# First products of gate and up: sums on VectorE, twelve early chunks, a late state update, and projection weights kept in DRAM as split pairs

## The chip, the cores and the metric

The kernel runs on one core of one Trainium2 chip. The metric is the device time of one execution in microseconds (us). Before the change it is 1289.85 us, the median of three runs (1289.18 to 1289.87).

## The reference, cut to what matters

One layer of a decoder is computed for 1024 new tokens of one sequence and for 8 running sequences of 4 tokens each, 1056 tokens in all, in float32:

```
proj = einsum('bld,dp->blp', h, w_in)                    # 1024 -> 2824 columns
o_a, S_new = gated_delta_rule(q, k, v, g, beta, S0)      # 4 heads, recurrent state S
o_b, k_new, v_new = swa_sinks(...)                       # sliding window, 8 query heads
m = concat[rmsnorm_gated(o_a, z), o_b] @ w_out
x = layernorm(ALPHA * x + m)                             # "LN1"
gate, up = split(x @ w_ffn_in)                           # 2 x 2816 columns
x = layernorm(ALPHA * x + (silu(gate) * up) @ w_ffn_out) # "LN2"
S = S * g_last + einsum('bhcd,bhce->bhde', k_dec, v_new) # the state that is handed back
```

## The kernel before, in words

**Tiles and stages.** Activations lie transposed: features on the 128 partitions, tokens along the free axis. The tokens are cut in two passes: s=0 with 512 tokens, s=1 with 544 (the other 512 and the 32 of the running sequences). The stages are: input projection of pass 0 and of pass 1 with convolution, delta rule and attention beside it (`mix_in`), output projection of both passes (`out_proj`), LN1, the gate and up products, the down products with LN2.

**Three products for one.** A float32 matmul is done as three fp32r matmuls. A weight piece of 128x512 (`wr`) is split by `Weights.split` into a high part `wh` (a cast on ScalarE, L162) and a low part `wl` (a subtraction on VectorE, L163), and TensorE does xh·wh + xl·wh + xh·wl. There are 4 buffers for `wh` and 4 for `wl`, so a piece can be split when TensorE has given back the piece four ahead of it, and 8 buffers for raw pieces, which SyncE's DMA queue fills ahead. Each projection weight is loaded and split twice, once in each pass. In pass 0 a dense product of 8 input tiles is 24 matmuls of 512 columns, in pass 1 it is 48 of 272 columns and goes through its two pieces twice, once for each half of the tokens.

**Gate and up.** These go by a scheme with seven products in place of eight: the 22 chunks `f` of (gate, up) have four quarters A11, A12, A21, A22 of weights and four blocks B11, B12, B21, B22 of LN1's output (first or second half of features, first or second half of tokens). GpSimd makes the sums S1 to S4 of the weights. The sums of the activations are made once, by `combine`: T1 = B12 - B11, T2 = B22 - T1, T3 = B22 - B12, T4 = B21 - T2, four tiles each, all split into a high and a low part (`split`, L1717 on ScalarE and L1718 on VectorE). A chunk is A11·B11, S2·T2, A12·B21, S3·T3, A22·T4, S1·T1, S4·B22, done by `product` (L1819 to L1821).

**The turn between LN1 and the chunks.** B11 and B21 need LN1 of pass 0 alone. So A11·B11 and A12·B21 of the first `NE` = 10 chunks are done early (`head`, `head2`), while LN1 of pass 1 and `combine` run on VectorE, ScalarE and GpSimd. Their results `x1`, `x2` are kept on the chip for two chunks and go to DRAM and back for the others (`xd`, `recall`). The main loop starts when the flag "T" says that all four sums of all four tiles are there.

**What sets the order.** Generators (`spawn`) hold the work beside the products; `pump` moves them on between products. A scheduler with a simulated clock then writes the order of every engine. Every engine runs its own list strictly in that order, so an instruction that waits holds up all behind it on its engine. This is so for SyncE too, which issues all DMAs.

**The state update.** At the end of `sample_delta` the state of the 8 running sequences is loaded again, `KM` (keys under a mask) times `vn` is added to the decayed state (matmuls L1427, VectorE L1432), and the result is stored. Only then the flag "sd" is set, for which `split_mix` (it splits the second pass's mixed heads for `out_proj(1)`) waits.

Of the kernel before, what the change touches and what calls it, by code (L numbers as in the profile page):

```python
# [80 lines left out]
NE = 10  # L81
# [3 lines left out]
L1 = (0, 1)  # L85
LE = 0
# [15 lines left out]
class Weights:  # L102
# [25 lines left out]
    def whole(self, ap):  # L128

        n = ap.shape[1]  # L130
        return [self.plain(self.raw(ap[:, c:min(c + 512, n)])) for c in range(0, n, 512)][0]

# [19 lines left out]
    def split(self):  # L152
# [5 lines left out]
        raw, done = self.make[i]()  # L158
        w = raw.shape[1]
        hi, lo = (k.wp.tile([P, 512], F32R, tag=t, bufs=NSPLIT, name=f"{t}{i}")[:, :w] for t in ("wh", "wl"))  # L160
        with k.tc.high_priority():
            nc.scalar.copy(hi, raw)  # L162
            nc.vector.tensor_tensor(lo, raw, hi.bitcast(F32), ALU.subtract)  # L163
        done()
# [44 lines left out]
def _program(k):  # L209
# [749 lines left out]
    ksT = cpt([P, 32], "ksT")  # L959
    vnew = cpt([P, P], "vnew")  # L960
# [301 lines left out]
    def sample_delta():  # L1262
# [144 lines left out]
        gl = small([P, 4, 8], "gl")  # L1407
        A.activation(gl.rearrange("p h b -> p (h b)"), pl[:, 0:32], AF.Exp)
        drop("ms")
        yield 200.0  # L1410
        yield from have("big")
        KM = bigt([P, 8, P], "KM")
        V.tensor_tensor(KM, bc(kd.unsqueeze(1), [P, 8, P]), bc(C["rowb"].unsqueeze(2), [P, 8, P]), ALU.mult)
        yield 0.0
        for b in (0, 4):
            yield from have("hp", 4)
            S0 = []
            for i in range(4):
                S0.append(page([P, 4, P], F32, f"S1_{b + i}"))
                dma(out=S0[i], in_=I["state"][b + i].rearrange("h k v -> k h v"))  # L1420
            yield 0.0
            yield from have("ms", 4)
            pu = [bank() for _ in range(4)]
            for i in range(4):
                for h in range(4):
                    o = slice(32 * h, 32 * h + 32)
                    mm(pu[h][:, i * P:(i + 1) * P], KM[o, b + i, :], vn[o, :], start=True, stop=True,  # L1427
                       tile_position=(32 * h, 0))
            yield 500.0
            for i in range(4):  # L1430
                for h in range(4):
                    V.scalar_tensor_tensor(S0[i][:, h, :], S0[i][:, h, :], gl[:, h, b + i:b + i + 1],  # L1432
                                           pu[h][:, i * P:(i + 1) * P], ALU.mult, ALU.add)
                dma(out=O["S_s"][b + i].rearrange("h k v -> k h v"), in_=S0[i])
                drop()
                if i % 2:
                    yield 0.0
            drop("ms", 4)
        drop("big")
        drop("hp", 3)  # L1440
        flags.add("sd")
# [50 lines left out]
    def layernorm(tiles, ssum, cw, gi, nm, done, lag=(0, 0), sums=None, bk="acc", order=range(8)):  # L1492
# [20 lines left out]
        for i, t in enumerate(tiles):  # L1513
# [14 lines left out]
            if i % 2 and not sums:  # L1528
                yield 0.0
# [19 lines left out]
        for j, i in enumerate(order):  # L1549
            t = tiles[i]  # L1550
            if j in PM:
# [5 lines left out]
            if j % 2:  # L1557
                yield 0.0
# [109 lines left out]

    for f in range(NE):
        q = quarters(f)  # L1670
        plan[f] = {n: W.plain(W.raw(q[n])) for n in ("A11", "A12")}
    for f in range(NF):
# [5 lines left out]
        for n in ("A11", "S2", "A12", "S3", "A22", "S1", "S4"):  # L1678
            if n in sm:
                p[n] = W.piece(*sm[n])  # L1680
            elif n not in p:
                p[n] = W.plain(r[n])
    wfo = I["w_ffo_t"]
# [36 lines left out]
    def ln1(gi, ssum):  # L1720
# [4 lines left out]
        def done(i, t):  # L1725
            dma(out=yd[i][:, SG[s][0] + c0:SG[s][0] + c0 + cw], in_=t)
            n = {(0, 0): "B11", (0, 1): "B21", (1, 1): "B22"}.get((s, i // 4))
# [4 lines left out]
        yield from layernorm([ac[s][d][:, cs] for d in range(8)], ssum, cw, 0, f"l1{gi}", done, L1, bk="acc" if gi else "ms",  # L1732
                             order=(0, 4, 1, 5, 2, 6, 3, 7) if s else range(8))
# [11 lines left out]
    def combine():  # L1745

        for i in range(4):
            yield from wait(*[("y1", g, j) for g in range(3) for j in (i, 4 + i)])
            b11, b21, b12, b22 = ac[0][i], ac[0][4 + i], ac[1][i], ac[1][4 + i]
            while not spare(8):  # L1750
                yield BLOCK
            t1, t3 = (take([P, HW_], F32, f"{n}raw{i}") for n in ("T1", "T3"))
# [5 lines left out]
            V.tensor_tensor(t1, b22, t1, ALU.subtract)  # L1758
            G.tensor_tensor(t3, b21, t1, ALU.subtract)
            split(*pair("T2", i, HW_), t1)  # L1760
            yield 0.0
            give(f"T1raw{i}")
            while not spare(2):
                yield BLOCK
            split(*(x[:, 0:512] for x in pair("T4", i, 512)), t3[:, 0:512])
            give(f"T3raw{i}")
            drop("hp", 4)
            yield 0.0
        flags.add("T")
# [35 lines left out]
    HALF = [(0, 272), (272, 544)]  # L1805

# [5 lines left out]
    def product(i, b, pss, start=True):  # L1812
        (wh, wl), = W.begin(i)
        for ps, c0, c1 in pss:
            o = ps[:, :c1 - c0]
            for kt in range(4):
# [5 lines left out]
                if c1 - c0 == 512 and kt == 1:  # L1822
                    W.step()
            if c1 == 272:
# [68 lines left out]
    for f in range(NE):  # L1893
        head(f)
        head2(f)
        if f >= NKEEP_X:
            for i in range(2):
                dma(out=xd[f][i], in_=X[f][i])
                give(f"x{i + 1}_{f}")

# [8 lines left out]
    need(lambda: "T" in flags)  # L1909
    for f in range(NF):  # L1910
# [193 lines left out]
```

## Time and profile before

| | |
|---|---|
| median of the runs | 1289.85 us |
| the profiled execution's own time | 1288.69 us |
| its span, first to last instruction | 1286.8 us |
| VectorE busy | 871.9 us (68%) |
| ScalarE busy | 616.2 us (48%) |
| GpSimd busy | 395.9 us (31%) |
| DMA moved | 170.81 MB, mean 133 GB/s |
| first output product starts | 419.87 us |
| first early product (B11) starts | 541.20 us |
| first down product starts | 1003.71 us |

How to read it: a busy time is the sum over an engine's instructions. TensorE's matmuls overlap, and their ends are modelled, so the pace of matmuls is read from the distance of their starts and not from their durations. The page cuts the span into 40 slices; a digit is the busy share in tenths, and the row PEclk is the share of its full clock that TensorE was granted. In a timeline, square brackets hold how long the engine had stood idle ahead of the instruction, and whose end ended that. The list of waits adds these up. A window row gives busy time (and number of instructions) of PE, PEld (weight load), DVE (VectorE), ACT (ScalarE) and POOL (GpSimd), then the granted clock, the share of the DMA engines' time and GB/s.

### The profile page before, as it was taken

Reading aid. Unit: us, or ns where it says so; the run is one execution under the profiler, and the core shown is the slowest. Engines: PE = TensorE matmul, PEld = TensorE weight load, DVE = VectorE, ACT = ScalarE, POOL = GpSimd, SP = SyncE. Lnnn points to the kernel's source line nnn. Section 1 sums busy time; section 2 is a strip of 40 time slices with the busy share of each in tenths; the row PEclk is TensorE's granted clock in tenths of the full one; section 3 lists DMA queues with packets and bytes.
Section 4 is the critical chain, followed back from the end, with each engine's and each line's share of the span. In section 5 each row is a group of like instructions: output and inputs, shape, how many; then the busy total and the mean of one; then the engine's idle time right before and its main releaser. Section 6 shows DMA issues by size and latency. Waiting matters only on the chain.

```text
span 1286.8 us, 24943 instructions
## 1 busy us (share of the span) xinstructions
PE 1248.8 (97%) x8701; PEld 1127.1 (88%) x8701; DVE 871.9 (68%) x1873; ACT 616.2 (48%) x1374; POOL 395.9 (31%) x1207
## 2 busy tenths in 40 slices
PE   9998999999999999996999999999999999999996
PEld 7887789999989888985999999999999998888995
DVE  6696975788885679868956655555655765622674
ACT  7674744757746433686322222322324554522453
POOL 1009411205722144437633433222332112201210
PEclk9999999999999999998999999999999999999999
DMA  7432341332133646444444422222324886733461
GB/s 252 138 90 70 93 133 39 104 120 83 45 116 105 193 140 205 157 155 155 167 155 141 147 92 74 76 83 75 112 86 119 295 269 190 214 100 114 143 218 47
DMA packets 119102, 170.81 MB, mean 133 GB/s; under 512 B 20272, under 2 KB 50096, under 8 KB 118960
## 3 DMA queue, kind: packets, MB, share of 16 engines
q1 hardware_dynamic: 118976, 169.22, 41.7%
q8 instruction: 68, 1.11, 0.3%
q14 instruction: 58, 0.48, 0.1%
HBM read 138.44 MB, written 31.75 MB: 132 GB/s over the span
## 4 chain that ended last, share of the span: by engine, by line
PE 48%; DVE 2%; DMA 1%; ACT 0%; issue 0%; DVEq 0%; SPq 0%; ACTq 0%; POOL 0%; POOLq 0%
PE acc L1990 6%; PE acc L1988 6%; PE acc L1989 6%; PE acc L1821 5%; PE acc L1819 5%; PE acc L1820 5%; PE ms L1819 5%; PE ms L1821 5%; PE ms L1820 5%; DMA hr<-hd 1%; DVE y L1554 1%; DVE wl L163 0%; PE ms L1522 0%; DMA wr<-in_w_ffo_t 0%; PE ms L1497 0%
## 5 line engine op out<-in xcount | busy, mean ns | idle before, releaser
L163 DVE TENSOR_TENSOR wl<-wr,wh 128x512 fp32r<-128x512 f32 x330 | 238.1, 725 | 141.0 <-ACT wh L162 131.6
L162 ACT CAST wh<-wr 128x512 fp32r<-128x512 f32 x330 | 197.2, 602 | 266.4 <-PE acc L1989 104.3
L433 PE MATMUL acc<-xh,wh 128*128 128x272 f32 (+1 forms) x528 | 174.5, 330 | 0.6 <-ACT qsm L1045 0.4
L434 PE MATMUL acc<-xl,wh 128*128 128x272 f32 (+1 forms) x528 | 173.7, 329 | 0.5 <-DVE xl L347 0.5
L435 PE MATMUL acc<-xh,wl 128*128 128x272 f32 (+1 forms) x528 | 173.6, 329 | 0.2 <-DVE wl L163 0.2
L1990 PE MATMUL acc<-hx,wl 128*128 128x272 f32 (+1 forms) x528 | 171.5, 325 | 1.5 <-DVE wl L163 1.4
L1988 PE MATMUL acc<-hx,wh 128*128 128x272 f32 (+1 forms) x528 | 171.8, 326 | 0.0
L162 ACT CAST wh<-S 128x512 fp32r<-128x512 f32 x88 | 54.4, 619 | 148.8 <-PE acc L1820 89.7
L1990 PEld LDWEIGHTS acc<-hx,wl 128*128 128x128 f32 x528 | 99.2, 188 | 10.6 <-DVE wl L163 2.4
L434 PEld LDWEIGHTS acc<-xl,wh 128*128 128x128 f32 x528 | 100.4, 190 | 8.9 <-issue 2.4
L433 PEld LDWEIGHTS acc<-xh,wh 128*128 128x128 f32 x528 | 100.4, 190 | 8.5 <-issue 1.0
L435 PEld LDWEIGHTS acc<-xh,wl 128*128 128x128 f32 x528 | 100.4, 190 | 8.0 <-issue 1.0
L1988 PEld LDWEIGHTS acc<-hx,wh 128*128 128x128 f32 x528 | 99.2, 188 | 8.2 <-issue 0.2
L1989 PE MATMUL acc<-hx,wh 128*128 128x272 f32 x352 | 101.5, 288 | 0.2 <-DVE hx L1718 0.2
L163 DVE TENSOR_TENSOR wl<-S,wh 128x512 fp32r<-128x512 f32 x88 | 72.2, 823 | 37.7 <-ACT wh L162 34.9
L1989 PE MATMUL acc<-hy,wh 128*128 128x512 f32 x176 | 69.4, 394 | 0.0
L1989 PEld LDWEIGHTS acc<-hx,wh 128*128 128x128 f32 x352 | 66.7, 189 | 0.7 <-DVE hx L1718 0.4
L433 PE MATMUL acc<-mh,wh 128*128 128x272 f32 (+1 forms) x192 | 64.0, 333 | 0.0
L434 PE MATMUL acc<-ml,wh 128*128 128x272 f32 (+1 forms) x192 | 63.3, 330 | 0.0
L435 PE MATMUL acc<-mh,wl 128*128 128x272 f32 (+1 forms) x192 | 63.1, 329 | 0.0
L1717 ACT CAST hx<-hr 128x272 fp32r<-128x272 f32 (+1 forms) x66 | 31.7, 486 | 46.1 <-DMA hr<-hd 41.5
L1659 POOL TENSOR_TENSOR S<-wr,S 128x512 f32<-128x512 f32 x22 | 34.8, 1581 | 53.4 <-DVE wl L163 53.4
(631 smaller groups left out, 3481.0 us busy)
## 6 DMA issues: line engine op xcount, KB each, us to landing
wr<-in_w_ffo_t SPq DMA_DIRECT2D x120, 256.0 KB, 3.0
wr<-in_w_ffi_t SPq DMA_DIRECT2D x108, 256.0 KB, 2.7
wr<-in_w_in_t SPq DMA_DIRECT2D x88, 256.0 KB, 2.6
wr<-in_w_out_t SPq DMA_DIRECT2D x32, 256.0 KB, 3.3
hd<-x SPq DMA_DIRECT2D x22, 272.0 KB, 2.7
hr<-hd SPq DMA_DIRECT2D x44, 136.0 KB, 2.8
hd<-x SPq DMA_DIRECT2D x22, 256.0 KB, 2.0
hr<-hd SPq DMA_DIRECT2D x22, 256.0 KB, 5.1
```

The lines of the kernel that those rows point to most:

```text
L162: nc.scalar.copy(hi, raw)
L163: nc.vector.tensor_tensor(lo, raw, hi.bitcast(F32), ALU.subtract)
L433: mm(ps[:, :cw], wh, xh[kt][:, c0:c0 + cw], start=(kt == 0), stop=False)
L434: mm(ps[:, :cw], wh, xl[kt][:, c0:c0 + cw], start=False, stop=False)
L435: mm(ps[:, :cw], wl, xh[kt][:, c0:c0 + cw], start=False, stop=(kt == n - 1))
L1659: G.tensor_tensor(t["S2"], W.get(r["A12"]), t["S2"], ALU.subtract)
L1819: mm(o, wh[:, kt, :], xh, start=(start and kt == 0), stop=False, **kw)
L1820: mm(o, wh[:, kt, :], xl, start=False, stop=False, **kw)
L1821: mm(o, wl[:, kt, :], xh, start=False, stop=(kt == 3), **kw)
L1988: mm(ps, wh[:, f % 4, :], xh, start=(f == 0), stop=False)
L1989: mm(ps, wh[:, f % 4, :], xl, start=False, stop=False)
L1990: mm(ps, wl[:, f % 4, :], xh, start=False, stop=(f == NF - 1))
```

## The change: what it does

1. *Projection weights as pairs in DRAM.* `twice` makes for each piece of `w_in` and `w_out` two tiles in DRAM. In pass 0 `split` stores `wh` and `wl` there right after the split (two DMAs of 128x512 for each of 44 + 16 pieces). In pass 1 there is no raw load, no cast and no subtraction: two DMAs fill `wh` and `wl`.
2. *Twelve early chunks.* `NE` is 12. Ten of them stand where the ten stood; chunk 10 stands behind S2·T2 of chunk 0, chunk 11 behind S3·T3. The wait for "T" becomes five waits, one for each of T2, T3, T4, T1 and B22's split.
3. *Sums on VectorE.* `combine` makes all four sums on VectorE (T1 and T4 were on GpSimd), first T2 with its split for each tile, then the splits of T3, T4, T1 and B22 in this order. LN1 of pass 1 does all its scaling on VectorE (two of eight tiles were on GpSimd) and yields after every tile; `product` pumps the generators once more in the middle of a 512-column product while the flag list `filling` is not empty.
4. *Late state update.* "sd" is set as soon as the decay factors are there. The update is a generator of its own (`state_update`), spawned when chunk 12 of the main loop is done, and works one head at a time with four matmuls each.

The diff, cut to its core:

```
-NE = 10
+NE = 12
+NBETWEEN = 2
@@ Weights.split
-        raw, done = self.make[i]()
+        raw, done = self.make[i]() if self.make[i] else (None, None)
...
+        if done:
+            with k.tc.high_priority():
+                nc.scalar.copy(hi, raw)
+                nc.vector.tensor_tensor(lo, raw, hi.bitcast(F32), ALU.subtract)
+            done()
+        for x, kept in zip((hi, lo), self.keep.get(i, ())):
+            nc.sync.dma_start(out=kept, in_=x.bitcast(F32))
+        for x, kept in zip((hi, lo), self.again.get(i, ())):
+            nc.sync.dma_start(out=x.bitcast(F32), in_=kept)
@@ sample_delta
-        KM = bigt([P, 8, P], "KM")
...
+        flags.add("sd")
+
+    def state_update():
+        kd, vn = late_state["nat"]
         for b in (0, 4):
+            while not spare(5):
+                yield BLOCK
+            KM = take([P, 4, P], F32, f"KM{b}")
...
+            for h in range(4):
+                yield from have("ms", 3)
+                pu = bank()
+                o = slice(32 * h, 32 * h + 32)
+                for i in range(4):
+                    mm(pu[:, i * P:(i + 1) * P], KM[o, i, :], vn[o, :], start=True, stop=True, tile_position=(32 * h, 0))
+                for i in range(4):
+                    V.scalar_tensor_tensor(S0[i][:, h, :], S0[i][:, h, :], gl[:, h, b + i:b + i + 1],
+                                           pu[:, i * P:(i + 1) * P], ALU.mult, ALU.add)
@@ combine
-            G.tensor_tensor(t1, b12, b11, ALU.subtract)
+            V.tensor_tensor(t1, b12, b11, ALU.subtract)
+            V.tensor_tensor(t2, b22, t1, ALU.subtract)
+            yield 0.0
             V.tensor_tensor(t3, b22, b12, ALU.subtract)
-            split(*pair("T3", i, HW_), t3)
+            split(*pair("T2", i, HW_), t2)
             yield 0.0
-            split(*pair("T1", i, HW_), t1)
-            V.tensor_tensor(t1, b22, t1, ALU.subtract)
-            G.tensor_tensor(t3, b21, t1, ALU.subtract)
...
+            V.tensor_tensor(t2, b21, t2, ALU.subtract)
...
+        flags.add("T2")
+        for n, j, w in (("T3", 2, HW_), ("T4", 1, 512), ("T1", 0, HW_), ("B22", 3, HW_)):
...
@@ main loop
-    need(lambda: "T" in flags)
+    need(lambda: "T2" in flags)
...
+        if f == 0:
+            early(NE - 2)
...
+        need(lambda: "T3" in flags)
...
+        if f == 0:
+            early(NE - 1)
+        need(lambda: "T4" in flags)
...
+        if f == NE:
+            spawn(state_update())
```

Three places show how the written order changes. The first is VectorE's list at the first T2 tiles. `T1raw`, `T2raw` and `T3raw` are sums before the split, an `l` behind a name is the low part, `mx` and `ac` are LN1's tiles, `wl` are weight splits. Before:

```order
L1718 TENSOR_TENSOR T3l_7876<-T3raw_7870,T3h_7874 128x544
L1718 TENSOR_TENSOR T1l_7907<-T1raw_7868,T1h_7905 128x544
L1758 TENSOR_TENSOR T1raw_7721<-mx_3506,T1raw_7721 128x544
L163 TENSOR_TENSOR wl_7998<-wr_7653,wh_7997 128x512
L1758 TENSOR_TENSOR T1raw_7868<-mx_3603,T1raw_7868 128x544
L1718 TENSOR_TENSOR T3l_7979<-T3raw_7973,T3h_7977 128x544
L1718 TENSOR_TENSOR T1l_8012<-T1raw_7971,T1h_8010 128x544
L163 TENSOR_TENSOR wl_8040<-wr_7690,wh_8039 128x512
L1718 TENSOR_TENSOR B22l_6724<-mx_4426,B22h_6722 128x272
L1718 TENSOR_TENSOR T2l_7780<-T1raw_7721,T2h_7778 128x544
```

And VectorE's list in the changed kernel, at its first T2 tile:

```order
L1789 TENSOR_TENSOR T1raw_7728<-mx_4223,ac_5994 128x544
L1792 TENSOR_TENSOR T3raw_7732<-mx_3679,mx_4223 128x544
L1752 TENSOR_TENSOR B22l_6754<-mx_3679,B22h_6752 128x544
L1790 TENSOR_TENSOR T2raw_7730<-mx_3679,T1raw_7728 128x544
L1583 TENSOR_TENSOR mx_4433<-mx_4433,l11y 128x272
L1583 TENSOR_TENSOR mx_4433<-mx_4433,l12y 128x272
L184 TENSOR_TENSOR wl_7852<-wr_7541,wh_7851 128x512
L1583 TENSOR_TENSOR mx_4575<-mx_4575,l11y 128x272
L1583 TENSOR_TENSOR mx_4575<-mx_4575,l12y 128x272
L1752 TENSOR_TENSOR B22l_6758<-mx_3774,B22h_6756 128x544
L184 TENSOR_TENSOR wl_7898<-wr_7578,wh_7897 128x512
L1752 TENSOR_TENSOR T2l_7752<-T2raw_7730,T2h_7750 128x544
```

The sums T1 and T2 now stand in VectorE's own list, amid LN1's scaling (`l11y`, `l12y`), and the first T2 tile is ready ahead of all but one split of T3 and T1, where before it came behind three of each.

The second place is TensorE's list, at the last matmuls of S2·T2 of chunk 0 (`T2l3` is the low part of its fourth tile; the two `ms` banks are the two halves of the tokens). Before:

```order
L1820 MATMUL acc_8243<-T4l1_7942,wh142_8141 128x512
L1821 MATMUL acc_8243<-T4h1_7940,wl142_8142 128x512
L1819 MATMUL ms_8162<-T2h3_8127,wh140_8070 128x272
L1819 MATMUL ms_8163<-T2h3_8127,wh140_8070 128x272
L1819 MATMUL acc_8243<-T4h2_8056,wh142_8141 128x512
L1820 MATMUL acc_8243<-T4l2_8058,wh142_8141 128x512
L1820 MATMUL ms_8162<-T2l3_8129,wh140_8070 128x272
L1821 MATMUL ms_8162<-T2h3_8127,wl140_8071 128x272
L1820 MATMUL ms_8163<-T2l3_8129,wh140_8070 128x272
L1821 MATMUL ms_8163<-T2h3_8127,wl140_8071 128x272
L1821 MATMUL acc_8243<-T4h2_8056,wl142_8142 128x512
```

After:

```order
L1863 MATMUL acc_8217<-B11h3_6732,wh141_8142 128x512
L1864 MATMUL acc_8217<-B11l3_6734,wh141_8142 128x512
L1865 MATMUL acc_8217<-B11h3_6732,wl141_8143 128x512
L1864 MATMUL ms_8182<-T2l3_7936,wh140_8105 128x272
L1865 MATMUL ms_8182<-T2h3_7934,wl140_8106 128x272
L1864 MATMUL ms_8183<-T2l3_7936,wh140_8105 128x272
L1865 MATMUL ms_8183<-T2h3_7934,wl140_8106 128x272
L1863 MATMUL acc_8132<-B21h0_6736,wh139_8060 128x512
L1864 MATMUL acc_8132<-B21l0_6738,wh139_8060 128x512
```

Before, the last T2 matmuls stand among T4's; now they stand between two early products, A11 of chunk 10 (`wh141`, `wl141`) and A12 of chunk 9 (`wh139`). 20 early products stand ahead of them.

The third place is SyncE's list in pass 1, where the decay rows of the delta rule (`R`, `Ball`, read back from `gd`) are loaded. Before:

```order
L598 DMA R_3079<-gd_3064 128x512
L601 DMA Ball<-gd_3064 128x512
L137 DMA wr_3452<-in_w_in_t 128x512
L998 DMA out_k_p<-kp 128x128
L999 DMA out_k_s<-kp 8x4x128
L137 DMA wr_3495<-in_w_in_t 128x512
```

After:

```order
L623 DMA R_3270<-gd_3255 128x512
L626 DMA Ball<-gd_3255 128x512
L189 DMA wh_3625<-wkh_105 128x512
L189 DMA wl_3626<-wkl_106 128x512
L189 DMA wh_3666<-wkh_107 128x512
L189 DMA wl_3667<-wkl_108 128x512
L189 DMA wh_3740<-wkh_109 128x512
L1025 DMA out_k_p<-kp 128x128
L1026 DMA out_k_s<-kp 8x4x128
L189 DMA wl_3741<-wkl_110 128x512
```

The raw loads, which fill eight buffers ahead of the splits, are gone; in their place stand the loads of the pairs, each of which waits until TensorE has given its buffer back.

More of the change, by code (lines that the diff above doesn't have):

```diff
@@ L112, in __init__ @@
         self.made = self.limit = 0
+        self.keep, self.again = {}, {}
     def raw(self, ap, uses=1):
@@ L131, in whole, with twice, second @@
         return [self.plain(self.raw(ap[:, c:min(c + 512, n)])) for c in range(0, n, 512)][0]
+    def twice(self, ap, n):
+        first = [self.whole(ap(t)) for t in range(n)]
+        for i in [j for f in first for j in (f, f + 1)]:
+            self.keep[i] = [self.k.dp.tile([P, 512], F32, name=f"wk{x}{i}") for x in "hl"]
+        def second():
+            out = []
+            for f in first:
+                for i in (f, f + 1):
+                    self.again[self.piece(None)] = self.keep[i]
+                out.append(len(self.make) - 2)
+            return out
+        return first, second
     def load(self, upto=1 << 30):
@@ L1443, in sample_read @@
+            for i in range(4):
+                dma(out=O["S_s"][b + i].rearrange("h k v -> k h v"), in_=S0[i])
+                give(f"S1_{b + i}")
+            give(f"KM{b}")
+            yield 0.0
+        drop("hp", 2)
     def sample_read(b, S0, WM, QM, vp, qp):
@@ L1489, in mix_in, with layernorm @@
         hook(1)
-    def layernorm(tiles, ssum, cw, gi, nm, done, lag=(0, 0), sums=None, bk="acc", order=range(8)):
+    def layernorm(tiles, ssum, cw, gi, nm, done, lag=(0, 0), sums=None, bk="acc", order=range(8), fine=False):
         def ones_mm(src):
@@ L1527, in layernorm @@
                 drop()
-            if i % 2 and not sums:
+            if (i % 2 or fine) and not sums:
                 yield 0.0
@@ L1667, in sums, with ahead @@
                 "S4": (last("S2", f"S2_{f}"), None)}
-    for f in range(NE):
+    def ahead(f):
         q = quarters(f)
-        plan[f] = {n: W.plain(W.raw(q[n])) for n in ("A11", "A12")}
+        plan.setdefault(f, {}).update({n: W.plain(W.raw(q[n])) for n in ("A11", "A12")})
+    for f in range(NE - NBETWEEN):
+        ahead(f)
     for f in range(NF):
@@ L1730, in done @@
             flags.add(("y1", gi, i))
[L1732 to L1733 removed]
+        yield from layernorm([ac[s][d][:, cs] for d in range(8)], ssum, cw, 0, f"l1{gi}", done, L1F if s else L1,
+                             bk="acc" if gi else "ms", order=(0, 4, 1, 5, 2, 6, 3, 7) if s else range(8), fine=s)
         flags.add(("y1", gi))
@@ L1892, in _program, with early @@
     xd = [[k.dp.tile([P, w], F32, name=f"xd{f}_{w}") for w in (HW_, 512)] for f in range(NE)]
-    for f in range(NE):
+    def early(f):
         head(f)
@@ L1899, in _program @@
                 give(f"x{i + 1}_{f}")
+    for f in range(NE - NBETWEEN):
+        early(f)
     def recall(f):
```

93 lines of the change are left out of this document (44 added, 49 removed).

## The prediction

> **What bounds the kernel now.** I read the page's busy times and slices first, to see which engine sets the time.
>
> ```profile
> span 1286.8 us, 24943 instructions
> PE 1248.8 (97%) x8701; PEld 1127.1 (88%) x8701; DVE 871.9 (68%) x1873; ACT 616.2 (48%) x1374; POOL 395.9 (31%) x1207
> PE   9998999999999999996999999999999999999996
> PEclk9999999999999999998999999999999999999999
> ```
>
> TensorE is busy 97% of the span. The change takes no matmul away, so all that can be won is time in which TensorE stands idle, 1286.8 - 1248.8 = 38 us, and time at a lower clock. Two slices of the PE row show 6: the last, which the change doesn't touch, and the nineteenth (about 579 to 611 us), where PEclk shows 8: the turn from the early products to the main loop. Windows of 5 us there, and two at the state update:
>
> ```profile
> 580.00:585.00 5.00, 4.34 (x19) 3.22 (x19) 1.60 (x3) 4.45 (x10) 1.86 (x8) 1.00 0.60 197
> 585.00:590.00 5.00, 2.65 (x9) 1.54 (x8) 4.64 (x4) 5.00 (x13) 5.00 (x7) 0.85 0.58 189
> 590.00:595.00 5.00, 5.00 (x20) 4.00 (x19) 5.00 (x7) 5.00 (x11) 3.57 (x11) 0.81 0.43 153
> 595.00:600.00 5.00, 2.05 (x7) 1.36 (x6) 5.00 (x9) 1.74 (x5) 1.58 (x1) 0.87 0.48 163
> 600.00:605.00 5.00, 3.50 (x13) 2.65 (x11) 4.31 (x8) 0.56 (x2) 5.00 (x1) 0.79 0.51 158
> 605.00:610.00 5.00, 1.99 (x5) 1.61 (x6) 3.55 (x3) 2.89 (x5) 4.99 (x11) 0.55 0.06 22
> 610.00:615.00 5.00, 5.00 (x27) 4.36 (x25) 5.00 (x5) 2.77 (x6) 4.12 (x16) 0.76 0.61 206
> 485.00:490.00 5.00, 3.53 (x25) 2.50 (x24) 5.00 (x14) 0.20 (x1) 0.48 (x8) 0.95 0.55 165
> 490.00:495.00 5.00, 5.00 (x31) 5.00 (x30) 5.00 (x18) 0.41 (x1) 1.16 (x25) 0.71 0.81 233
> ```
>
> The first figure after the window's length is PE's busy time. From 580 to 615 us PE is idle for 0.66 + 2.35 + 0 + 2.95 + 1.50 + 3.01 + 0 = 10.5 us. The clock column adds busy time times the missing share: 2.65·0.15 + 5·0.19 + 2.05·0.13 + 3.50·0.21 + 1.99·0.45 + 5·0.24 = 4.5 us. So the turn costs 15.0 us. At the state update the same sum gives 1.47 us idle and 3.53·0.05 + 5·0.29 = 1.6 us of clock, 3.1 us.
>
> The list of waits says whom PE waited for at these places and in pass 1's input projection:
>
> ```profile
> PE acc L1819 <- ACT x L1880: 5.2, 2, 4.5
> PE acc L1821 <- DVE wl L163: 4.5, 2, 2.9
> PE ms L1427 <- DVE S L1432: 1.5, 2, 0.9
> PE ms L992 <- ACT junk L668: 2.3, 1, 2.3
> PE ms L754 <- DVE hs L699: 2.0, 1, 2.0
> PE ms L563 <- ACT gt L554: 1.1, 1, 1.1
> ```
>
> The first two are the turn: an early result that ScalarE had not taken out of its bank, and weight splits that VectorE had not done. Both are short jobs stuck in a queue, as the timeline shows:
>
> ```profile
> 595.37 0.71 DVE L1718 TENSOR_TENSOR T1l<-T1raw,T1h 128x544 fp32r<-128x544 f32 x1
> 596.00 0.43 DVE L1718 TENSOR_TENSOR B22l<-mx,B22h 128x272 fp32r<-128x272 f32 x1
> 596.35 0.71 DVE L1718 TENSOR_TENSOR T3l<-T3raw,T3h 128x544 fp32r<-128x544 f32 x1
> 598.26 0.68 DVE L163 TENSOR_TENSOR wl<-wr,wh 128x512 fp32r<-128x512 f32 x1
> 598.86 0.71 DVE L1758 TENSOR_TENSOR T1raw<-mx,T1raw 128x544 f32<-128x544 f32 x1
> 619.46 1.17 DVE L1718 TENSOR_TENSOR T2l<-T1raw,T2h 128x544 fp32r<-128x544 f32 x1 [0.92 <-ACT T2h L1717]
> 598.42 7.08 POOL L1759 TENSOR_TENSOR T3raw<-ac,T1raw 128x544 f32<-128x544 f32 x1 [3.84 <-DVE T1raw L1758]
> 605.53 0.62 ACT L1717 CAST T4h<-T3raw 128x512 fp32r<-128x512 f32 x1 [4.96 <-POOL T2l L229]
> 607.38 0.58 ACT L1880 COPY x<-acc 128x512 f32<-128x512 f32 x1
> ```
>
> GpSimd's sum for T4 takes 7.08 us; ScalarE's cast of T4 waits 4.96 us for GpSimd, and the copy L1880 that PE waits for stands behind the cast. The last T2 tile is split at 619.5 us. So the bound at the turn is the queues of VectorE and ScalarE, not the matmuls.
>
> **The change part by part.**
>
> *Sums on VectorE, twelve chunks.* What VectorE must do until the last T2 tile is split is counted from its written list, from the first subtraction of the mean of pass 1 on. The steps are distances of starts in the rows above: 596.00 to 596.35, 0.35 us for 272 columns; 595.37 to 596.00, 0.63 us for 544; 598.26 to 598.86, 0.60 us for 512. There are 48 of 272 columns (LN1), 29 of 544 (sums and splits) and 19 of 512 (17 weight splits, 2 of T4): 16.8 + 18.3 + 11.4 = 46.5 us.
>
> ```profile
> 545.19 1.48 DVE L1514 TENSOR_TENSOR mx<-mx,acc 128x272 f32<-128x272 f32 x4
> 545.00:580.00 35.00, 35.00 (x153) 28.42 (x152) 24.70 (x56) 28.05 (x53) 12.25 (x35) 1.00 0.46 155
> 541.20 0.40 PE L1819 MATMUL acc<-B11h,wh 128*128 128x512 f32 x1
> 553.24 0.39 PE L1819 MATMUL acc<-B11h,wh 128*128 128x512 f32 x1
> 558.77 0.40 PE L1819 MATMUL acc<-B21h,wh 128*128 128x512 f32 x1
> 644.03 0.25 PE ms L1819 x2
> 658.79 0.25 PE ms L1819 x2
> ```
>
> That work starts at 545.2 us. In the LN1 stretch VectorE stood idle 35.0 - 24.7 = 10.3 us, waiting for ScalarE and for the splits that PE paces; I keep this. So T2 is ready at 545.2 + 46.5 + 10.3 = 602.0 us.
>
> PE's side: an early product of 12 matmuls took 558.77 - 553.24 = 5.53 us for two, 2.77 us. The four products from 541.20 to 553.24 took 12.04 us, 1.0 us more than 4·2.77: LN1's mean. I take 1.0 us again for the two variances. A chunk of the main loop is 658.79 - 644.03 = 14.76 us, of which 12 matmuls are wide, so the other 96, of 272 columns, take 0.125 us each. Ahead of the last four T2 matmuls PE has 20 early products and 20 T2 matmuls: 541.2 + 2.0 + 55.3 + 2.5 = 601.0 us. So PE comes 1 us too early; since both queues also wait for each other in between, I take 3 us of wait, and clock in the proportion of the turn before, 4.5/10.5: 1.3 us more. 4.3 us stay of 15.0, a gain of **10.7 us**. Bounds: nothing stays (15.0), or 6 us of wait with 2.6 of clock (6.4).
>
> Behind the last T2 split VectorE has some 6 us of work to T4's last split (two T1, two T4, three weight splits, a sum, the take-out of T2's product). PE has A12 of chunk 9, S3·T3, A12 of chunk 10 and A11 of chunk 11 there, 3·2.77 + 3.0 = 11.3 us; so T3, T4 and T1 cost nothing. If T2 alone were covered and this not, the next wait would be up to 6 us. The two more chunks cost no matmul; their spill, reload and second load of A11 and A12 lie beside the main loop. GpSimd keeps only the sums of weights there.
>
> *State update.* Its wait goes, **3.1 us**, with 32 VectorE steps and a KM product out of a stretch where VectorE was busy all the time (windows 485 to 495). In the main loop the same matmuls come back:
>
> ```profile
> 479.43 1.73 PE L1427 MATMUL ms<-sov,KM 32*128 32x128 f32 x32
> ```
>
> 32 in 1.73 us with four row groups in turn, 0.05 us each; the new order takes one row group at a time. Bounds for the 64 records: 0.05 us again (no loss), or the 0.125 us of the 272-column ones (64·0.075 = 4.8 us more). I take **1.0 us**, near the first, since the load is of 32 rows and not of 128. The 32 VectorE steps lie beside PE. Net 2.1 us, bounds +3.1 and -1.7.
>
> *Pairs in DRAM.* Pass 1 loses 60 casts and 60 subtractions, so ScalarE and VectorE come sooner to what PE waits for: 2.3 + 2.0 + 1.1 = 5.4 us in the rows above. I take a third, 1.8 us, since these three stand behind other work too. Against it, a pair must now land between the return of its buffer and its use.
>
> ```profile
> wr<-in_w_in_t SPq DMA_DIRECT2D x88, 256.0 KB, 2.6
> R<-gd SPq DMA_DIRECT2D x8, 256.0 KB, 5.4
> 420.00:460.00 40.00, 39.92 (x363) 34.28 (x362) 27.11 (x75) 16.72 (x50) 7.24 (x50) 1.00 0.71 213
> ```
>
> A dense product of pass 1 is 48·0.125 = 6.0 us. The first piece's buffers are free after three quarters of it and are needed again when the next one has ended: 1.5 + 6.0 = 7.5 us. Two issues of some 0.5 us and 2.6 us of landing are 3.6 us, with the 5.4 us of a crowded queue 6.4 us. So it fits, barely at worst; I take 0.8 us of waits. Net gain **1.0 us**, bounds +5.4 and the rival below. The 120 stores of pass 0 (31 MB) hold no one: a buffer is filled again four pieces later, 11 us or more.
>
> *Sum.* 10.7 + 2.1 + 1.0 = 13.8 us off the profiled execution's own 1288.69 us: 1274.9 us. That execution lay 1.2 us below the median of the runs, 1289.85, so the median should be **1276 us**.
>
> [...] In the rows at 585 to 595 us the granted clock is 0.85 and 0.81 when PE had stood idle 2.35 us in that window. [...]
>
> **The rivals.** (a) *VectorE stays the bound of the turn.* It now makes eight more sums of 0.63 us and LN1's scaling; if its idle time grows as it waits for splits, 8.6 us stay as in the bound: 1280 us. For it: 46.5 us against 55 us of cover leaves little. 16 in 100. (b) *All bounds are good*: 15.0 + 3.1 + 5.4 = 23.5 us, 1266 us. Against it: LN1's chain of mean, squares, variance remains. 13 in 100. (c) *The clock doesn't fall for a short wait*: 1.3 us less, 1275 us. For it, the wait is shorter than most of the turn's; against it, the rows named. 15 in 100. (d) *Slower: pairs come late.* SyncE's list holds the pairs behind loads that wait for other engines (the eight R and Ball loads, the inverse, masks, mixed heads), and at 420 to 460 us DMA is busy 0.71 already, before the stores of `w_out`. If landing passes 6.5 us, each pair costs PE the rest. Priced at 0.3 us for 60 pieces, 18 us: 1294 us. It decides from 0.23 us a piece (13.8/60) on. 12 in 100. (e) *No effect*, since TensorE's own order moves its waits elsewhere: 1290 us. 4 in 100.
>
> **How the numbers follow.** The forecast has 40 in 100. A measurement of this kernel can tell about 0.2% (2.6 us) from no change. Faster by more: forecast, (a), (b), (c), 0.84. Within: (e) and a little of (d), 0.05. Slower: 0.11. The range takes in (b) and goes up to just short of no change: 1266 to 1288 us.
>
> **What would show it.** Right: in the profile after, windows of the turn with PE full but for a few us, no GpSimd sum in it, the last T2 split near 602 us, no PE wait at the state update, matmuls of KM in the main loop with no wait ahead of them. Wrong: PE waits for DMA pairs in pass 1 or `out_proj(1)`, a clock below 1 there, or a second long wait at T2 for VectorE. If the turn is filled and the time is not near 1276 us, the projections are where to look.

## The result, and the profile after

The changed kernel took 1280.08 us, the median of four runs (1277.81 to 1282.33), beside 1289.86 us before (four runs, 1289.18 to 1291.03): a ratio of 0.9926, with a 95% interval of 0.9907 to 0.9945. On another chip, beside seven runs of the kernel before, it took 1279.91 us, a ratio of 0.9909 (0.9894 to 0.9923). The forecast was 1276 us, 13.8 us fewer than before; measured are 9.8 us fewer in the first comparison, 11.5 us in the second, and 10.9 us between the two profiled executions (1288.69 and 1277.81 us). The sum of gains was 2 to 4 us too high. Its three terms missed in different directions, and two of them by as much as the sum or more: that the total came out near the forecast is partly luck.

The page of the changed kernel, with the same rows as were read of before:

```profile
span 1276.0 us, 25111 instructions
PE 1246.0 (98%) x8701; PEld 1127.2 (88%) x8701; DVE 817.1 (64%) x1822; ACT 584.3 (46%) x1310; POOL 372.1 (29%) x1205
PE   9999999989999999998999999999999999999996
PEclk9999999999999999999999999999999999999998
```

The two weak digits of the turn (6 in PE, 8 in PEclk) are gone; an 8 is left there. VectorE works 55 us less and ScalarE 32 us less, with 60 weight pieces fewer to split. Where the 10.8 us of span went is read from the first starts of four groups of matmuls. In these rows the two times behind the durations are the first and the last start, in us:

```profile
L458 PE MATMUL acc<-xh,wh x528: 282/289/628, 6.4 to 414.9; 128*128 128x272 f32 x117, 128*128 128x512 f32 x59
L458 PE MATMUL acc<-mh,wh x192: 283/289/579, 415.3 to 528.3; 128*128 128x272 f32 x128, 128*128 128x512 f32 x64
L1863 PE MATMUL acc<-B11h,wh x88: 387/393/653, 528.6 to 974.4; 128*128 128x512 f32 x88
L2049 PE MATMUL acc<-hx,wh x528: 282/288/597, 992.6 to 1259.0; 128*128 128x272 f32 x117, 128*128 128x512 f32 x59
```

The same groups start at 6.0, 419.9, 541.2 and 1003.7 us before. The distances cut the span into stages, and the same was done for every kernel below (one profiled execution each):

| stage (us) | before | changed | again | e1 | e2 | e3 | e4 | e5 | e6 | e7 | e8 | e9 | e10 | e11 |
|---|---|---|---|---|---|---|---|---|---|---|---|---|---|---|
| input projection, both passes | 413.9 | 408.9 | 409.2 | 414.2 | 409.8 | 410.5 | 411.4 | 407.9 | 412.7 | 409.4 | 410.8 | 410.0 | 408.8 | 408.3 |
| output projection | 121.3 | 113.3 | 113.3 | 113.7 | 121.8 | 122.0 | 113.4 | 113.4 | 113.7 | 113.3 | 113.4 | 113.3 | 113.3 | 113.4 |
| early products, turn, main loop | 462.5 | 464.0 | 464.0 | 463.4 | 455.4 | 462.4 | 465.2 | 462.3 | 473.6 | 465.5 | 463.4 | 463.7 | 460.1 | 458.7 |
| down products, LN2 | 283.1 | 283.4 | 283.7 | 285.9 | 287.2 | 284.2 | 287.8 | 284.4 | 286.0 | 286.9 | 283.7 | 284.0 | 284.9 | 284.4 |

"Again" is the changed kernel once more, e1 to e11 are the experiments. The change gives 5.0 us in the input projection and 8.0 us in the output projection; the long stage behind them, which holds the turn, got 1.5 us longer, although the turn itself got better: the late state update, which now lies in it, costs 10.2 us, as the experiments show. The last row is a warning: no edit touches the down products, and they differ by up to 4.7 us from one profile to another. The span of one profile can't tell 3 us here; the stages can.

The turn, in the same windows of 5 us (PE's busy time first behind the length, the clock third from the end):

```profile
570.00:575.00 5.00, 4.51 (x20) 3.35 (x20) 5.00 (x10) 5.00 (x11) 0.40 (x6) 1.00 0.93 293
580.00:585.00 5.00, 1.36 (x6) 0.75 (x4) 2.42 (x5) 1.80 (x4) 4.64 (x10) 1.00 0.11 38
585.00:590.00 5.00, 4.28 (x13) 3.08 (x14) 5.00 (x9) 3.61 (x7) 1.56 (x5) 0.66 0.64 206
595.00:600.00 5.00, 4.82 (x25) 3.92 (x24) 5.00 (x8) 3.75 (x8) 1.95 (x8) 1.00 0.63 204
```

All other windows from 570 to 605 us are full at clock 1.00. Idle are 0.49 + 3.64 + 0.72 + 0.18 = 5.0 us, and the clock takes 4.28·0.34 = 1.5 us: 6.5 us in place of 15.0. The same sums in the other profiles give 14.3 and 14.4 us in e3 and e6, which leave VectorE's sums and the early chunks as before, and 5.7 to 8.4 us in all the others. So the gain at the turn belongs to these two parts of the change. Which of their pieces gave it (the sums moved, T2 first, the finer steps) no run separates; e7 below takes back the two added chunks alone. The list of waits shows what TensorE waited for; the second and the third row stand in pass 1 and pass 0 of the input projection:

```profile
PE ms L1863 <- ACT wh L183: 4.0, 1, 4.0
PE ms L1019 <- ACT junk L693: 3.1, 1, 3.1
PE ms L1148 <- DVE st L1133: 2.1, 1, 2.1
PE acc L1863 <- ACT x L1926: 1.0, 3, 0.5
PE acc L458 <- DMA wh<-wkh: 0.3, 1, 0.3
```

So one wait of 4.0 us is left at the turn, and it isn't for VectorE: it is for the high part of a weight tile. The last row is all that TensorE waited for a pair from DRAM. Followed back in the timeline, the wait of 4.0 us leads to GpSimd:

```profile
577.13 5.97 POOL L1677 TENSOR_TENSOR S<-wr,wr 128x512 f32<-128x512 f32 x1
583.04 0.10 POOL L254 MEMSET S<- 128x1 f32 x1
583.07 0.10 POOL L254 MEMSET T4h<- 128x1 f32 x1
583.21 1.27 POOL L1678 TENSOR_TENSOR S<-S,wr 128x512 f32<-128x512 f32 x1
581.26 0.72 DVE L1795 TENSOR_TENSOR T2raw<-ac,T2raw 128x544 f32<-128x544 f32 x1
584.55 0.69 DVE L1752 TENSOR_TENSOR T4l<-T2raw,T4h 128x512 fp32r<-128x512 f32 x1 [2.58 <-POOL T4l L254]
583.20 0.62 ACT L1751 CAST T4h<-T2raw 128x512 fp32r<-128x512 f32 x1 [4.79 <-POOL T4h L254]
584.75 0.60 ACT L183 CAST wh<-S 128x512 fp32r<-128x512 f32 x1
585.40 0.39 PE L1863 MATMUL ms<-T2h,wh 128*128 128x272 f32 x1 [4.04 <-ACT wh L183]
```

Read it from the bottom. S2·T2 waits for its weights' cast at 584.75, which waits for S2 = S1 - A11 on GpSimd (583.21), which stands behind S1 = A21 + A22 (577.13). The same kind of sum takes 1.27 us in one row and 5.97 us in the other. VectorE worked without a break until 581.98 us, and the long sum ended 1.1 us after that, at 583.10. While it stood, the memsets behind it stood too: every buffer that is taken gets a short memset from GpSimd first (L254), so ScalarE waited 4.79 us for T4's buffer and VectorE 2.58 us. The trace of before had the same case: GpSimd's sum of 7.08 us began at 598.42 while VectorE worked without a break, until 604.31, and ended at 605.50. But not every sum on GpSimd stands under a busy VectorE. A little earlier in the trace of before it was VectorE that waited:

```profile
591.25 1.55 POOL L1648 TENSOR_TENSOR S<-wr,wr 128x512 f32<-128x512 f32 x1
591.57 1.82 DVE L1718 TENSOR_TENSOR T3l<-T3raw,T3h 128x544 fp32r<-128x544 f32 x1
```

There GpSimd's sum took 1.55 us, and the split that VectorE took up in the meantime needed 1.82 us in place of 0.71. What decides which of the two waits, no run here shows: both this sum and the one of 5.97 us started 0.32 us behind a VectorE sum (590.93 and 576.81).

### The profile page after: what moved, and what is told of

Its sections match the earlier page's. It is cut to its first block, busy times and chain, and to the rows that moved or that the text cites. A ratio compares the mean times of both kernels' runs of the same rounds, so it can differ in the third digit from the quotient of the medians.

```text
span 1276.0 us, 25111 instructions
## 1 busy us (share of the span) xinstructions
PE 1246.0 (98%) x8701; PEld 1127.2 (88%) x8701; DVE 817.1 (64%) x1822; ACT 584.3 (46%) x1310; POOL 372.1 (29%) x1205
## 4 chain that ended last, share of the span: by engine, by line
PE 58%; DVE 2%; DMA 2%; ACT 2%; issue 1%; POOL 0%; DVEq 0%; ACTq 0%; SPq 0%; POOLq 0%
PE acc L2051 6%; PE acc L1863 6%; PE acc L2049 6%; PE acc L2050 6%; PE acc L1865 6%; PE acc L1864 6%; PE ms L1863 5%; PE ms L1865 5%; PE ms L1864 5%; PE acc L460 2%; PE acc L459 2%; PE acc L458 2%; DMA hr<-hd 1%; PE ms L1459 1%; DVE y L1583 1%
## 5 line engine op out<-in xcount | busy, mean ns | idle before, releaser
L183 ACT CAST wh<-wr 128x512 fp32r<-128x512 f32 (+1 forms) x270 | 160.7, 599 | 230.6 <-PE acc L2050 104.6
L184 DVE TENSOR_TENSOR wl<-wr,wh 128x512 fp32r<-128x512 f32 (+1 forms) x270 | 188.6, 702 | 121.0 <-ACT wh L183 109.7
L2051 PEld LDWEIGHTS acc<-hx,wl 128*128 128x128 f32 x528 | 99.2, 188 | 10.9 <-DVE wl L184 2.8
L1863 PE MATMUL ms<-T2h,wh 128*128 128x272 f32 x176 | 50.8, 290 | 4.0 <-ACT wh L183 4.0
L1863 PE MATMUL acc<-T3h,wh 128*128 128x272 f32 x176 | 50.8, 289 | 0.0
```

Of the source, the lines that this page charges most:

```text
L1863: mm(o, wh[:, kt, :], xh, start=(start and kt == 0), stop=False, **kw)
L2051: mm(ps, wl[:, f % 4, :], xh, start=False, stop=(f == NF - 1))
```

## The experiments

**e1, e3: the pairs taken away, and the pairs alone.** e1 is the changed kernel without the pairs, e3 the kernel before with nothing but them.

```
-    for n, ap, order in (("in", "w_in_t", TILES), ("out", "w_out_t", range(8))):
-        idx[n + "0"], second = W.twice(lambda j: I[ap][order[j]], len(order))
-        idx[n + "1"] = second()
+    for n, ap, order in (("in0", "w_in_t", TILES), ("in1", "w_in_t", TILES), ("out0", "w_out_t", range(8)),
+                         ("out1", "w_out_t", range(8))):
+        idx[n] = [W.whole(I[ap][t]) for t in order]
```

> The changed kernel, with each projection weight loaded raw and split again in pass 1, as before the change. Theory: the pairs gave most of what the stages ahead of the early products gained beyond the state update (first output product 4.6 us earlier, and about 1.5 us in the output projection), so without them 6 us come back: about 1286 us, with the first output product near 420 us again. Rival: that gain came from the order that the scheduler happened to write, or from the moved update, and the pairs are worth what the prediction gave them, 1 us: about 1281 us. Second rival: the pairs cost time and something else gained more: under 1279 us.

> The kernel before with the pairs in DRAM and nothing else of the change. Theory: 5 to 6.5 us fewer than before, about 1284 us, all of it ahead of the early products; the turn to the main loop keeps its 15 us. Rival: 1 us as predicted, 1289 us. Second rival: pairs come late without the rest of the change, over 1290 us, with waits of TensorE for the pair loads.

Measured: e1 1286.68 us, 0.9958 of before (0.9942 to 0.9975), against 0.9909 to 0.9926 with the pairs; e3 1287.19 us, 0.9971 (0.9957 to 0.9984), which is 3.9 us fewer than the 1291.1 us beside it. By stages: the input projection takes 407.9 to 411.4 us in the kernels with pairs and 412.7 to 414.2 us in the three without (before, e1, e6), so the pairs give 4 us there. In the output projection they give nothing: 113.7 us without beside 113.3 us with them, 121.3 beside 122.0. The theory's size fits e1 and was too high for e3 (3.9 us, not 5 to 6.5); its share for the output projection (1.5 us) was wrong. The longest wait for a pair in any of the lists was 1.9 us, once each in e2 and e3, in the output projection:

```profile
PE ms L1015 <- ACT junk L691: 2.6, 1, 2.6
PE ms L1144 <- DVE st L1129: 2.1, 1, 2.1
PE acc L458 <- DMA wl<-wkl: 1.9, 1, 1.9
PE ms L777 <- DVE Dl L769: 1.6, 1, 1.6
```

That is e3. The waits for `hs` and `gt` that stood in the list of before are gone, new ones (`st`, `Dl`) have come.

**e6, e2: the late update alone, and the update put back.** e6 is the kernel before with only the late state update, e2 the changed kernel with the update in its old place and form.

```
+        late_state["nat"] = kd, vn
+        drop("hp", 1)
+        flags.add("sd")
...
+    def state_update():
...
+        if f == 12:
+            spawn(state_update())
```

> The kernel before with the late state update and nothing else of the change. Theory, from the stages of the earlier runs: the output projection gets 8 to 8.5 us shorter and the main loop 8.6 to 10.2 us longer, so the time stays within 2 us of before. Rival, the prediction's sum: 2.1 us fewer, with a main loop about 4 us longer.

> The changed kernel, with the state update back in the output projection, in its old form. Theory: in the main loop the 64 matmuls of the update cost 10.2 us (two chunks of 25.3 and 25.4 us, two of 20.34 us each expected), early they and their wait cost 6.3 us; so the time falls by about 4 us, to 1276 us, the two long chunks are gone and the first early product starts 6 us later. Rival: the prediction's own sum, by which the late update is worth 2.1 us: 1282 us.

Measured: e6 1295.91 us, 1.0041 of before (1.0026 to 1.0056): slower, by 4.7 us of the medians. The stages say the same with less: 7.6 us fewer in the output projection, 11.1 us more behind it. Two chunks of the main loop take 25.33 and 25.63 us where the others take 20.35, so 10.3 us are the update's own. In the changed kernel, the first matmul of B22 in chunks 12, 13 and 14 of the main loop, and one step of the update between them:

```profile
802.65 0.29 PE L1863 MATMUL ms<-B22h,wh 128*128 128x272 f32 x1
827.93 0.29 PE L1863 MATMUL ms<-B22h,wh 128*128 128x272 f32 x1
853.51 0.29 PE L1863 MATMUL ms<-B22h,wh 128*128 128x272 f32 x1
808.03 0.29 PE L1865 MATMUL ms<-T2h,wl 128*128 128x272 f32 x1
808.25 1.15 PE L1459 MATMUL ms<-sov,KM 32*128 32x128 f32 x8
809.34 0.50 PE L1863 MATMUL acc<-B21h,wh 128*128 128x512 f32 x1
```

25.28 and 25.58 us, again 10.2 us above two times 20.34. Eight records of one row group (four matmuls, two records each) take 809.34 - 808.25 = 1.09 us, 0.135 us each. The eight steps make 8.7 us of the 10.2; the rest, some 0.2 us a step, goes at the changes between these and the other matmuls: the last matmul ahead of each step and the first one behind it have some 0.1 us more to the next start (0.21 to 0.22 us ahead, 0.23 us behind, where 0.125 us is the distance for 272 columns).

e2 did not give the 4 us that the theory gave it: 1283.47 us, 0.9937 (0.9918 to 0.9955). The two long chunks are gone and the stage is 8.6 us shorter, but the output projection is 8.5 us longer, and in e2's profile the turn lost 8.4 us (5.5 idle, 2.9 of clock) instead of 6.5, with a wait of 3.1 us for the same weights and one of 1.8 us for those of an early product. So in the changed kernel early and late cost the same within what can be told. The early form cost 8 us and not the 6.3 that I had counted for e2's expectation.

**e5, e10: row groups in turn.** In the changed kernel each step does four matmuls of one head, all in one row group of TensorE. e5 does four heads in turn as the kernel before did, with four banks; e10 two heads in turn, with two banks:

```
-            for h in range(4):
-                yield from have("ms", 3)
-                pu = bank()
...
+            for hh in (0, 2):
+                yield from have("ms", 4)
+                pu = [bank() for _ in range(2)]
                 for i in range(4):
...
+                    for h in (hh, hh + 1):
```

> The changed kernel, with the late state update's matmuls in the old order: four banks, the four row groups in turn, instead of four matmuls in a row in one row group. Theory: the price of the late update, 10.2 us for 64 matmuls, is that each waits for the weights of its own row group; in turn they take 0.05 us each, so two chunks of about 22.5 us instead of 25.4 us, and the time falls by 5 to 6 us against the changed kernel. Rival: the price is the change between the update's narrow matmuls and the wide ones, or VectorE's 32 steps: less than 2 us fewer.

> The changed kernel, with the late update working on two heads at a time: two banks, eight matmuls that change between two row groups. With all four heads the scheduler had put two fifths of them in one row group in a row again, and those took 0.135 us a record as in the changed kernel, while those in turn took 0.068 us. Theory: all 64 records at 0.068 us and four switches instead of eight: the update costs the main loop 5 to 6 us instead of 10.2, so about 4.5 us fewer than the changed kernel. Rival: the gain of rows in turn is taken by a lower clock or by VectorE behind it: under 2 us fewer.

Measured: e5 1277.76 us, 0.9893 (0.9874 to 0.9911), beside 0.9909 (0.9894 to 0.9923) for the changed kernel on the same chip: 1.6 thousandths, 2 us, with intervals that overlap, and in the stage 1.7 us. Neither the theory's 5 to 6 us nor a clear win for the rival: the scheduler wrote the third and fourth head's matmuls in a row again, so that 24 of the 64 records still ran at 0.135 us, and the clock was halved from 809.70 to 813.11 us, behind the first step. With two banks the order held. e10's steps:

```profile
809.53 1.17 PE L1460 MATMUL ms<-sov,KM 32*128 32x128 f32 x16
810.63 0.50 PE L1865 MATMUL acc<-B21h,wh 128*128 128x512 f32 x1
813.60 1.16 PE L1460 MATMUL ms<-sov,KM 32*128 32x128 f32 x16
814.69 0.39 PE L1865 MATMUL acc<-T3h,wh 128*128 128x272 f32 x1
```

Sixteen records in 1.09 us, 0.068 us each: a step now does twice the work in the time of the changed kernel's, and there are four steps instead of eight. The two chunks take 20.86 and 24.99 us, 5.2 us over instead of 10.2, the stage 460.1 us instead of 464.0, and the time is 1275.55 us, 0.9882 (0.9862 to 0.9902). The theory's 4.5 us came as 3.9 us in the stage. So half of the late update's price was the single row group; the other 5.2 us remain.

**e4, e8, e9: what holds the turn.** e4 makes two of the four weight sums of chunk 0 on VectorE, e8 all four, e9 keeps besides the early results of one chunk on the chip instead of two, which leaves two more buffers.

```
+        E = G if f else V
...
-            G.tensor_tensor(t["S1"], a["A21"], a["A22"], ALU.add)
-            G.tensor_tensor(t["S2"], t["S1"], a["A11"], ALU.subtract)
+            E.tensor_tensor(t["S1"], a["A21"], a["A22"], ALU.add)
+            E.tensor_tensor(t["S2"], t["S1"], a["A11"], ALU.subtract)
...
-NKEEP_X = 2
+NKEEP_X = 1
```

> The changed kernel, with the sums S1 and S2 of chunk 0's weights made on VectorE instead of GpSimd. Theory: at the turn TensorE waited 4 us for the weights of S2, whose sum took GpSimd 5.97 us while VectorE was busy without a break, and lost 1.5 us of clock after it; on VectorE the two sums take 1.3 us. What is late next is the last T2 split, some 3 us behind its first use: a gain of 2 to 4 us, about 1277 us. Rival: T2's splits bound the turn as much as the weights did, and two more sums in VectorE's list delay them: 1280 to 1282 us.

> The changed kernel with all four sums of chunk 0's weights on VectorE, so that GpSimd has no sum in the turn, only its short memsets. Theory: a GpSimd sum stands still while VectorE works without a break (5.97 and 5.41 us where 1.3 us is its time alone), and all that stands behind it in GpSimd's list stands too, buffer memsets for which ScalarE's copies wait; with none there the turn loses 2 to 3 us instead of 6.5 us, against 1.3 us of VectorE work: 3 to 4 us fewer than the changed kernel. Rival: the memsets wait for pages that stores to DRAM have to free, and the turn keeps its 6 us: no change.

> The changed kernel with the four sums of chunk 0's weights on VectorE, and with the early results of one chunk kept on the chip instead of two, which leaves two more buffers free in the turn. Theory: with the sums gone from GpSimd, TensorE waited 3.3 us for an early result's copy on ScalarE that stood behind a T4 cast, and that cast waited for a buffer which a store to DRAM had to free; with two more buffers the wait at this place shrinks to under 1.5 us, and the turn loses some 3 us instead of 6.6. Rival: the next store is as late as the one before, and the wait stays over 2.5 us.

Measured: e4 1283.55 us, 0.993 (0.9907 to 0.9953): no gain. The wait for the weights is gone from its list, and another stands in its place, 5.9 us for ScalarE's copies of early results. The third sum had become the one that stands:

```profile
591.55 5.41 POOL L1689 TENSOR_TENSOR S<-wr,S 128x512 f32<-128x512 f32 x1 [0.53 <-DVE wl L184]
596.93 0.13 POOL L254 MEMSET x<- 128x1 f32 x2
595.13 0.69 DVE L184 TENSOR_TENSOR wl<-wr,wh 128x512 fp32r<-128x512 f32 x1
598.07 0.58 ACT L1927 COPY x<-acc 128x512 f32<-128x512 f32 x1
598.70 0.50 PE L1864 MATMUL acc<-B21h,wh 128*128 128x512 f32 x1 [2.12 <-ACT x L1927]
```

VectorE's run ends at 595.82, the sum 1.14 us later, then the buffer's memset, then the copy, then TensorE. It is the third case with the same distance. The turn loses 7.5 us (5.9 idle, 1.6 of clock). e8, without any sum on GpSimd there: 1278.69 us, 0.9898 (0.9882 to 0.9915), stage 463.4 beside 464.0: no gain that the intervals can tell. The turn still loses 6.6 us (3.8 idle, 2.9 of clock), with one wait that has a new cause:

```profile
582.08 0.10 POOL L254 MEMSET T4h<- 128x1 f32 x1 [2.55 <-DMA xd<-x]
582.32 0.62 ACT L1752 CAST T4h<-T2raw 128x512 fp32r<-128x512 f32 x1 [2.38 <-POOL T4h L254]
585.42 0.58 ACT L1927 COPY x<-acc 128x512 f32<-128x512 f32 x1 [0.40 <-POOL x L254]
586.06 0.80 PE L1864 MATMUL acc<-B21h,wh 128*128 128x512 f32 x1 [3.25 <-ACT x L1927]
```

T4's buffer is one that the store of an early result (`xd`) has to free; the cast of T4 waits for it, the copy stands behind the cast in ScalarE's list, and TensorE behind the copy. This is the rival: buffers that stores have to free, not GpSimd's sums, were the next bound. e9, with two more buffers: 1278.44 us, 0.9906 (0.9885 to 0.9928), stage 463.7. Its two waits at the turn:

```profile
PE acc L1864 <- ACT x L1927: 2.2, 2, 1.7
PE ms L1864 <- POOL x L1924: 1.9, 1, 1.9
```

The wait of 3.3 us went, two of 1.9 and 1.7 us came; the turn loses 5.7 us (4.2 idle, 1.6 of clock). The theory's 3 us were not reached. Three edits took away three causes in a row, and each time other waits took their place: the turn loses 7.5, 6.6 and 5.7 us, where the changed kernel loses 6.5.

**e7: none between.** The changed kernel with ten early chunks, none between the products of chunk 0 (`NE = 10`, `NBETWEEN = 0`).

> The changed kernel with ten early chunks as before and none between the products of chunk 0. Theory: the turn waits for the weight sums on GpSimd and for buffers, not for the splits of T3, T4 and T1, which were done by 598 us, so the two chunks in between cover little: within 2 us of the changed kernel. Rival, from the prediction: behind T2 there are 6 us of splits to cover, so without the two chunks up to 6 us more.

Measured: 1281.32 us, 0.9922 (0.9908 to 0.9937), beside 0.9909 (0.9894 to 0.9923): the intervals overlap. Its turn holds the same 4.0 us wait for the weights and 1.3 us for copies, 5.3 us idle as in the changed kernel, and 2.8 us of clock instead of 1.5. No wait for a split of T3, T4 or T1 came up. The two chunks in between cover nothing that these runs can tell.

**e11: all three** (e9 and e10 together), and the changed kernel beside e5, e7 and e8:

> The changed kernel with all three: the first chunk's sums on VectorE, one chunk's early results kept, two rows in turn in the late update. Theory: the gains add, 3 to 4 us at the turn and 4.5 us in the main loop: about 7 us fewer than the changed kernel, 0.985 to 0.987 of the kernel before. Rival: the turn keeps its 6 us and only the update's gain is left: about 0.989.

> The changed kernel itself, once more, beside the next three on the same chip. All theories: about 0.993 of the kernel before, 1280 to 1283 us, since single runs of one kernel lay up to 9 us apart and the down products alone, which nothing here touches, took 283 to 288 us in the profiles.

Measured: 1272.64 us, 0.9863 (0.9838 to 0.9887), the fastest of all. The update's gain is all there; of the turn's, 0.8 us by the windows and 1.4 us by the stage. The turn loses 5.7 us, all of it idle time, with the clock at 1.00 throughout. It beats both kernels: its interval lies below the changed kernel's, and it takes 18.6 us fewer than the kernel before beside it.

## Why the prediction was right, and where its steps failed

**What bounds the kernel.** Right: the matmuls are the same 8701 records, and all that moved is idle time, clock, and the pace of the 64 small matmuls.

**The turn: 10.7 us forecast, 8.5 us measured** (15.0 to 6.5), within the bounds of 6.4 and 15.0. The mechanism held: the waits for T1's and T4's sums on GpSimd are gone, and so is the one for a weight split on VectorE. The step that failed is the one that said "GpSimd keeps only the sums of weights there", and gave them no price: the first of them, S1, stood 5.97 us, and most of what is left is the wait for S2. I had the row for it before me, the sum of 7.08 us, and read it as the price of T4's sum instead of a price that a GpSimd sum could have under VectorE's full list. In the trace S1 stood not for one instruction of VectorE but for the rest of VectorE's run as a whole (5.97 us for 1.27 us, to 1.1 us behind the run's end); in the pair of rows of before at 591 us it is VectorE that stood, in one split beside one sum (1.82 us for 0.71). The count of VectorE's own work was fair: the last T2 split was forecast 60.8 us after the first early product and ended at 594.2 us, 65.6 us after it; it kept TensorE waiting nowhere, since the wait for S2 lay ahead of it. That it would have been late without that wait is what e11 hints at, with 0.4 us for T2's low part.

**The state update: 2.1 us fewer forecast; about 2 us more measured, and in e6 4.7 us more.** This is the worst step. The price of a matmul record was taken near 0.05 us "since the load is of 32 rows and not of 128". They took 0.135 us in one row group, more than my upper bound of 0.125, and some 0.2 us more at each of eight steps: 10.2 us in all instead of 4.2. e10 shows that the row group makes half of it: two groups in turn, 0.068 us a record, 5.2 us in all. My reason for the low price was wrong: in the changed kernel's trace, records of 128 columns that follow each other start 0.111 us apart over 128 rows (median of 739) and 0.112 us apart over 32 rows in one row group (median of 56), and the load of a 32-row matmul of the update took 0.187 us (median of 64), that of a 128-row one beside it 0.19 us. In part the error was hidden, because the early update was dearer too: 8 us of the output projection, where I had 6.3 (3.1 of wait and clock, 3.2 of matmuls).

**Pairs in DRAM: 1.0 us fewer forecast, 4 us measured,** near the bound of 5.4. The step that failed is "I take a third"; and the 0.8 us that I set against it were 0.3 us. What I named as the gain is only half seen: `hs` and `gt` went from the list, but the wait for `junk` grew from 2.3 to 3.1 us, and idle time and clock explain only 2.1 of the 5.0 us that lie between the two traces in the input projection (11.7 and 9.7 us idle, 6.8 us at half clock in both). Which of the many small waits gave the rest stays open. The reason why no pair came late holds: TensorE waited 0.3 us for pairs in the changed kernel, and the 31 MB of stores hold nothing up: from 20 to 100 us TensorE is busy 20.00 of 20 us in every window.

**Sum and rivals.** By stages: -5.0, -8.0, +1.5, +0.3 us, and 0.4 us later start, the 10.8 us of the span. The forecast's terms were -10.7, -2.1, -1.0; measured they are about -8.5, +2, -4 to -5: the pairs made up for about half of what the other two fell short. That part was luck. Rival (a), VectorE as the bound of the turn at 1280 us, gave the time that was measured, but not by its mechanism. Rival (d), pairs late, didn't come. Rival (c), that a short wait costs no clock, was wrong here (1.5 us of clock behind the wait of 4.0 us) and right in e11, as shown below.

## What to carry to other kernels

When work is moved off a queue, price what stays in that queue too, under the load that the move creates: GpSimd's remaining sum stood 5.97 us, until VectorE's fuller list had a gap. Here small matmuls of 32 rows in one row group took twice the time that they took in two groups in turn (0.135 and 0.068 us a record), and moving them out of a stall into a full loop cost more than the stall (by 4.7 us in e6). Cut the span into stages by first starts before believing a total: here a stage that no edit touches moved by 4.7 us.

## What the runs showed of the hardware that was not expected

Some GpSimd sums stood until a run of VectorE ended: 1.1, 1.1 and 1.2 us after that run in the three kernels shown (5.97 and 5.41 us for 128x512, 7.08 us for 128x544), where the one at 583.21 us took 1.27 us. In the traces of before and of the changed kernel 248 sums of these shapes stand. Three of them took more than 3 us (7.08, 5.97 and 3.26 us), and each of the three ended 1.12 to 1.19 us after VectorE's run did. Most were not held: the median is 1.32 us before and 1.30 us in the changed kernel.

What the clock did after a wait of TensorE did not follow from the wait's length alone. In the traces of before and of the changed kernel its records change 18 times between 20 and 1262 us, from 1.00 to 0.50 and back, in each trace on one grid of 3.41 us, and the changes go with how much of the grid window before it TensorE was busy. The windows at full clock that were busy for 12 to 43% were followed by one at 0.50 in 8 of 8 cases; of two that were busy for 56% and 61%, the second was; of 706 that were busy for more, none. In e5 such a full window, the one that ends at 809.70 us, was followed by one at 0.50, which stays unexplained. So in these runs it mattered where on the grid a wait fell. In e9 a wait of 1.92 us lies within one grid window (the first row; the clock is the third figure from the end):

```profile
580.94:584.35 3.41, 1.49 (x9) 1.04 (x8) 3.41 (x7) 2.19 (x5) 0.48 (x8) 1.00 0.63 216
584.35:587.77 3.42, 3.42 (x10) 2.64 (x10) 3.42 (x7) 2.37 (x5) 0.29 (x3) 0.50 0.21 81
```

In e11 waits of 1.94 and 2.83 us are each cut in two by an edge of the grid, and the clock stays at 1.00:

```profile
578.88:582.29 3.41, 1.80 (x8) 1.13 (x6) 3.41 (x7) 2.09 (x4) 0.36 (x7) 1.00 0.69 199
582.29:585.70 3.41, 3.08 (x15) 2.62 (x16) 3.41 (x7) 3.35 (x7) 0.45 (x5) 1.00 0.38 142
595.94:599.36 3.42, 1.74 (x8) 1.43 (x9) 1.24 (x3) 2.38 (x5) 0.32 (x5) 1.00 0.48 146
599.36:602.77 3.41, 3.41 (x24) 3.18 (x23) 2.89 (x5) 1.90 (x4) 1.48 (x4) 1.00 0.80 226
```

TensorE is busy 44% of the window in e9, 53% and 51% in e11, so these cases lie where either was seen. My 1.3 us of clock for a wait of 3 us, set in proportion, was a fair mean of what these traces show and no more: there the price came in grid windows at 0.50, which cost up to 1.7 us each (3.41/2), or not at all.
